# Norm statistics of two MLPs moved to a pinned place, GpSimd out of layer 1's projection, and the last square root on ScalarE

## The chip, the core and the metric

The kernel runs on one core of a Trainium2 chip, launched once. The metric is the device time of one execution in microseconds. The core's engines are TensorE (PE; PEld is its weight load), VectorE (DVE), ScalarE (ACT), GpSimd (POOL) and SyncE (SP, which issues the transfers here). Each engine runs its own instructions in their written order and waits at an instruction until what it needs is there.

## What is computed

A stream of 256 tokens of width 1024 goes through two blocks one after the other. All is float32. Cut to what matters here:

```python
def first_block(x, ...):
    for layer in range(2):
        h = rmsnorm(x, mix_norm[layer])
        if layer == 0:
            y = mixer_ab(h, ...)     # gated convolution beside attention
        else:
            y = mixer_c(h, ...)      # convolution, gated linear recurrence, projection c_w_out
        x = x + y
        x = x + sq_relu_mlp(rmsnorm(x, mlp_norm[layer]), w_up[layer], w_down[layer])
    return rmsnorm(x, final_norm)

def second_block(x, c, ctx, ...):
    h  = rmsnorm_2(x, norm_g) * (1 + scale) + shift      # shift, scale, gate from c and w_mod
    hc = rmsnorm_2(ctx, norm_g) * (1 + scale_c) + shift_c
    ...                                                  # two attentions over x and ctx
    y = (sigmoid(ga) * ya + sigmoid(gb) * yb) @ w_out
    return rmsnorm_2(x + gate * y, final_g)
```

`rmsnorm` divides a token by the root of the mean of its squares; `sq_relu_mlp` is `square(relu(h @ w_up)) @ w_down` with 4096 inner columns.

## The kernel before

Activations stand transposed: 128 channels on the partitions, 256 tokens along the row, eight such blocks for the width of 1024. Weights are read as 236 units of 128 x 1024 (512 KB) in the order of use. Each float32 operand is split into a rounded high half and the low half that is left, and a product is three matmuls (`mm3`, L383 to L385: high by high, low of the input by high, high by low of the weight), so a unit is 24 matmuls of 256 columns.

`fetch` issues a unit's transfer into one of four staging buffers (`raw`, `RAW = 4`). `prep` makes the halves: the high one (`wh`, or `wxh` where the second ring of buffers is in use) by ScalarE (L323) or by a cast on VectorE, the low one (`wl`, `wxl`) by VectorE or GpSimd (both L326). The table `POLICY` says for each kind of unit which engines do it: "av" is ScalarE then VectorE, "ag" ScalarE then GpSimd, "vv" VectorE for both. `unit` hands the next unit to a matmul loop and prepares units ahead; `more(n)` prepares n more at that place. `split` and `lo` (L435) do the same for activations.

An MLP (`mlp`) goes over 16 pairs of 256 inner columns. `up(p)` multiplies pair p; ScalarE applies ReLU (`mr`) and squares it into the high half (`mah`), GpSimd squares it again (`ma`, L989), VectorE takes the low half (`mal`). From pair 2 on, two rows of the down projection (of pair p - 2) follow each pair, summed in four accumulators. The norm of the MLP is applied at the end as its square, since ReLU squared is quadratic: `ssq` (L444, L445: ScalarE squares, GpSimd adds and folds) makes the channel sums of squares, `csum` (L452) sums over the partitions with two small matmuls, `meaneps` and a reciprocal give the factor, and `spread` multiplies it out over the partitions (L470) and copies it (`R2`).

During the first MLP VectorE also computes the conditioning vectors (`mod_setup`: L906 makes `cv`, L915 are 40 products with `w_mod`), hung in between as background steps; during the second one the context is normed the same way (`ctx_setup`, which calls `ssq` on `cx` in the same pool, where the tile `ssum` has one buffer).

Layer 1 (`layer1`) pins the order on TensorE and ScalarE between `conv` and `wrow(4)`. Gates, root (L1103), scan (L1108), GELU (L1115) and product (L1119, `done`) of four pairs of channel blocks alternate with the projections; then `wrow(k)` multiplies rows 0 to 4 of the output projection "wo1", and `proj_tail` rows 5 to 7, block pair by block pair, adding to `x` and making the next input halves `xsh` and `xsl`. Two of the four accumulators of "wo1" come free when VectorE has read `acc` at L1099.

At the end (`b2_out`) the squares of the result are summed by small matmuls into `st`; VectorE makes mean plus EPS (L458), GpSimd raises it to -0.5 (L463), TensorE spreads it (L470), VectorE multiplies, and five transfers write the output.

Tile schedules the instructions of every engine by itself unless `inorder` or `issue_after` fixes them; so a step that is written in one place may stand elsewhere in an engine's order.

## Time and profile before

| | before |
|---|---|
| median of 3 runs | 824.75 us (823.21 to 827.11) |
| profiled execution | 821.14 us |
| its span, first to last instruction | 819.4 us |
| granted TensorE clock, mean | 0.991 |
| TensorE busy | 787.9 us (96%) |
| VectorE busy | 576.4 us (70%) |
| ScalarE busy | 473.2 us (58%) |
| GpSimd busy | 199.0 us (24%) |

The table's last rows are shares of the span. A busy TensorE is not a TensorE at its peak, since matmuls overlap. Times in the views count from the start of the span. A share over the whole span says little of one stage; a stage is read from its own stretch of the timeline.

### The profile page before, as it was taken

What the parts mean: (1) busy time and instruction counts of PE and PEld (TensorE: products, weight loads), DVE (VectorE), ACT (ScalarE), POOL (GpSimd) and SP (SyncE); (2) the same over time, 40 slices, a digit from 0 to 9 for tenths busy, and PEclk for the clock granted to TensorE, in tenths of its full rate; (3) what the DMA queues carried; (4) which work ended last, traced back from release to release, by engine and by line L of the source; (5) the groups of instructions that cost most, each with busy time, mean ns of one, the idle gap of its engine ahead of it and who ended that gap; (6) DMA issues with size and microseconds to landing.
All of it is one profiled execution on the core that took longest, in us unless ns stands there. A gap on an engine that the chain in (4) does not pass through costs nothing.

```text
span 819.4 us, 16154 instructions
## 1 busy us (share of the span) xinstructions
PE 787.9 (96%) x6480; PEld 756.0 (92%) x6480; DVE 576.4 (70%) x952; ACT 473.2 (58%) x739; POOL 199.0 (24%) x151
## 2 busy tenths in 40 slices
PE   6999989999999999979999999999999999999996
PEld 5997889999999999978999999999989988889996
DVE  6999669999989787578746545557634877565843
ACT  5568656455545657877745444445626587765533
POOL 4796643011101202330531110111000022320001
PEclk9999999999999999999999999999999999999997
DMA  7874357787988832238726656664335533555531
GB/s 239 292 222 130 103 181 247 292 311 272 322 307 283 286 113 88 62 124 302 239 99 210 193 189 190 197 196 164 94 119 151 159 105 102 176 163 176 185 101 52
DMA packets 41259, 152.32 MB, mean 186 GB/s; under 512 B 4576, under 2 KB 5088, under 8 KB 39008
## 3 DMA queue, kind: packets, MB, share of 16 engines
q1 hardware_dynamic: 40752, 149.19, 55.5%
q10 hardware_dynamic: 432, 2.10, 0.7%
q8 instruction: 51, 0.84, 0.4%
q14 instruction: 24, 0.20, 0.1%
HBM read 149.17 MB, written 2.10 MB: 185 GB/s over the span
## 4 chain that ended last, share of the span: by engine, by line
PE 59%; issue 19%; DVE 8%; ACT 8%; POOL 4%; DMA 2%; SPq 0%; POOLq 0%; DVEq 0%; ACTq 0%
PE mm L383 10%; PE mm L384 10%; PE mm L385 10%; PE acc L384 7%; PE acc L383 7%; PE acc L385 7%; POOL ma L989 3%; PE acc L1423 2%; PE acc L1451 2%; PE mm L1460 2%; ACT wh L323 1%; DMA raw<-in_wst 1%; DVE wl L326 1%; PE mm L470 1%; DMA x<-in_xT 1%
## 5 line engine op out<-in xcount | busy, mean ns | idle before, releaser
L323 ACT ACTIVATE wh<-raw 128x1024 fp32r<-128x1024 f32 (+1 forms) x190 | 198.3, 1048 | 162.5 <-PE mm L384 64.2
L326 DVE TENSOR_TENSOR wl<-raw,wh 128x1024 fp32r<-128x1024 f32 (+1 forms) x159 | 197.6, 1250 | 100.1 <-ACT wh L323 98.3
L383 PE MATMUL mm<-xsh,wh 128*128 128x256 f32 x752 | 210.4, 280 | 0.0
L384 PE MATMUL mm<-xsl,wh 128*128 128x256 f32 x752 | 209.1, 278 | 0.0
L385 PE MATMUL mm<-xsh,wl 128*128 128x256 f32 x752 | 209.1, 278 | 0.0
L383 PEld LDWEIGHTS mm<-xsh,wh 128*128 128x128 f32 x752 | 141.7, 188 | 3.7 <-issue 3.3
L384 PEld LDWEIGHTS mm<-xsl,wh 128*128 128x128 f32 x752 | 141.7, 188 | 0.6 <-DVE xsl L878 0.2
L385 PEld LDWEIGHTS mm<-xsh,wl 128*128 128x128 f32 x752 | 141.3, 188 | 0.0
L989 POOL TENSOR_TENSOR ma<-mr 128x512 f32<-128x512 f32 x32 | 49.5, 1548 | 246.2 <-ACT mr L987 246.2
L384 PE MATMUL acc<-mal,wh 128*128 128x256 f32 x360 | 100.1, 278 | 1.0 <-DVE mal L435 1.0
L383 PE MATMUL acc<-mah,wh 128*128 128x256 f32 x360 | 100.3, 279 | 0.0
L385 PE MATMUL acc<-mah,wl 128*128 128x256 f32 x360 | 100.0, 278 | 0.0
L326 POOL TENSOR_TENSOR wl<-raw,wh 128x1024 fp32r<-128x1024 f32 x31 | 74.2, 2414 | 43.8 <-ACT wh L323 43.8
L323 ACT ACTIVATE wxh<-raw 128x1024 fp32r<-128x1024 f32 x47 | 49.2, 1055 | 38.8 <-DMA raw<-in_wst 34.9
L384 PEld LDWEIGHTS acc<-mal,wh 128*128 128x128 f32 x360 | 67.9, 189 | 1.2 <-DVE mal L435 1.2
L383 PEld LDWEIGHTS acc<-mah,wh 128*128 128x128 f32 x360 | 67.7, 188 | 0.0
L385 PEld LDWEIGHTS acc<-mah,wl 128*128 128x128 f32 x360 | 67.6, 188 | 0.0
L326 DVE TENSOR_TENSOR wxl<-raw,wxh 128x1024 fp32r<-128x1024 f32 x44 | 56.6, 1299 | 8.0 <-ACT wxh L323 8.0
L384 PE MATMUL mm<-xsl,wxh 128*128 128x256 f32 x208 | 58.1, 279 | 0.6 <-DVE xsl L878 0.6
L383 PE MATMUL mm<-xsh,wxh 128*128 128x256 f32 x208 | 58.3, 280 | 0.0
L385 PE MATMUL mm<-xsh,wxl 128*128 128x256 f32 x208 | 58.0, 279 | 0.0
L915 DVE CUSTOM_DVE_ANT_0 mdump<-mw,cv 128x1024 f32<-128x1024 f32 x40 | 48.7, 1217 | 2.7 <-DMA mw<-in_modw 2.6
(386 smaller groups left out, 1855.9 us busy)
## 6 DMA issues: line engine op xcount, KB each, us to landing
raw<-in_wst SPq DMA_DIRECT2D x240, 512.0 KB, 4.1
mw<-in_modw SPq DMA_DIRECT2D x12, 1024.0 KB, 7.2
nb<-in_nab SPq DMA_DIRECT2D x16, 256.0 KB, 3.7
ab<-in_alibi ACTq DMA_DIRECT2D x1, 1536.0 KB, 8.9
x<-in_xT SPq DMA_DIRECT2D x4, 256.0 KB, 4.9
cv<-in_cvec SPq DMA_DIRECT2D x1, 1024.0 KB, 4.7
cx<-in_cT SPq DMA_DIRECT2D x1, 1024.0 KB, 7.3
xd<-x SPq DMA_DIRECT2D x1, 1024.0 KB, 4.6
```

Of the source, the lines that this page charges most:

```text
L323: nc.scalar.activation(wh, r, AF.Copy)
L326: (nc.vector if lo == "v" else nc.gpsimd).tensor_tensor(wl, r, wh.bitcast(F32), op=ALU.subtract)
L383: mm(out, w[0], x[0], start=start, stop=False, skip_group_check=True)
L384: mm(out, w[0], x[1], start=False, stop=False, skip_group_check=True)
L385: return mm(out, w[1], x[0], start=False, stop=stop, skip_group_check=True)
L470: self.lasts = self.nc.tensor.matmul(ps[:, j * 128:(j + 1) * 128], rc[:, j:j + 1].to_broadcast([128, 128]), self.ident, start=True, stop=True)
L915: V.tensor_tensor_reduce(d, w, cv[:, s * 1024:(s + 1) * 1024], 0.5, 0.0, op0=ALU.mult, op1=ALU.add, accum_out=self.mod[:, s * 24 + i:s * 2 ...
L989: G.tensor_tensor(a, r, r, op=ALU.mult)
L1423: PE.matmul(sc[i], Q[tag, h][a][:, qs], K[tag, h][b], start=a + b == 0, stop=a == 1)
L1451: PE.transpose(pt[:, i * 128:(i + 1) * 128], P[:, i * 128:(i + 1) * 128], self.ident)
L1460: PE.matmul(o[64 * hh:64 * hh + 64, :T], vt[:, i, h * 64:h * 64 + 64], PTs[tag, h][:, i], start=i == 0, stop=i == 3, skip_group_check=True)
```

## The change

- `POLICY["wo1"]`: rows 0 to 2 get both halves from VectorE, rows 3 to 7 ScalarE and VectorE; before, rows 0 to 3 were ScalarE and GpSimd.
- In `layer1` the products `done(2)` and `done(3)` are written right after rows 0 and 1, and the units prepared there are put behind the low half that `done` makes.
- In `mlp` the squares of `x` are written at pair 1 (before: 4), their sum over the partitions and the reciprocal at pair 3 (before: 6), the spread before the second down row of pair 4 (before: at pair 8). TensorE's order in pairs 3 and 4 is pinned, and what those pairs issue afterwards is put behind the reciprocal.
- The spread of the final gain (`R1`) moves from the output stage to the end of `b2_kv`.
- At the end ScalarE takes the square root of mean plus EPS, ahead of the last four scalings; VectorE takes the reciprocal. The table with the root is loaded early, behind the last tanh.

```diff
--- before.py
+++ after.py
@@ -45,7 +45,7 @@
 POLICY.update(val=("av", "ag", "av", "ag"), gate=("av", "av", "av", "ag"), xr=("av",), ri=("av",), cg=("av", "av", "av", "av", "ag", "ag", "ag", "ag"))
 POLICY["wo0"] = ("ag",) * 7 + ("av",)
 POLICY["up"] = ("ag",) * 4 + ("av",) * 60
-POLICY["wo1"] = ("ag",) * 4 + ("av",) * 4
+POLICY["wo1"] = ("vv",) * 3 + ("av",) * 5
 PADC = 30
 
 COLS = {}
@@ -432,7 +432,7 @@
         self.nc.vector.scalar_tensor_tensor(l, xs, g, h.bitcast(F32), op0=ALU.mult, op1=ALU.subtract)
 
     def lo(self, l, src, h):
-        self.nc.vector.tensor_tensor(l, src, h.bitcast(F32), op=ALU.subtract)
+        self.lastlo = self.nc.vector.tensor_tensor(l, src, h.bitcast(F32), op=ALU.subtract)
 
     def ssq(self, pool, x3):
         nc = self.nc
@@ -1000,17 +1000,22 @@
                 self.ahead = min(2 * p - 14, 13)
             if l == 1 and p == 4:
                 self.wx, self.slot = None, 0
-            up(p)
-            if p == 4:
-                parts = self.ssq(mp, x)
-            if p == 6:
-                v = self.meaneps(self.csum(parts), D)
-                rv = self.t(self.cp, [128, 2], "rv")
-                V.reciprocal(rv, v)
-            if p == 8:
-                R2 = self.spread(mp, rv, "R2")
-            if p >= 2:
-                for k in (2 * p - 4, 2 * p - 3):
+            with ExitStack() as order:
+                if p == 3 or p == 4:
+                    order.enter_context(self.inorder(PE.engine))
+                if p == 4:
+                    order.enter_context(self.tc.issue_after(ri_.ins))
+                up(p)
+                if p == 1:
+                    parts = self.ssq(mp, x)
+                if p == 3:
+                    v = self.meaneps(self.csum(parts), D)
+                    rv = self.t(self.cp, [128, 2], "rv")
+                    ri_ = V.reciprocal(rv, v)
+                    order.enter_context(self.tc.issue_after(ri_.ins))
+                for k in (2 * p - 4, 2 * p - 3) if p >= 2 else ():
+                    if k == 5:
+                        R2 = self.spread(mp, rv, "R2")
                     self.krow(acc, self.unit("down"), A.pop(k), k == 0, False)
         for k in range(28, 32 - NT):
             self.krow(acc, self.unit("down"), A.pop(k), False, False)
@@ -1162,13 +1167,17 @@
             gelu(3)
             self.more(2)
             acc = [self.ps("acc") for _ in range(4)]
-            for k in range(4):
-                if k == 2:
-                    done(2)
-                if k == 3:
-                    done(3)
+            wrow(0)
+            done(2)
+            with self.tc.issue_after(self.lastlo.ins):
+                self.more(1)
+            wrow(1)
+            done(3)
+            with self.tc.issue_after(self.lastlo.ins):
+                self.more(2)
+            for k in (2, 3):
                 wrow(k)
-                self.more(1 if k == 0 else 2)
+                self.more(2)
             wrow(4)
         self.ahead = 2
         xs = self.new_h()
@@ -1360,6 +1369,7 @@
                 V.scalar_tensor_tensor(cf[:, k], cf[:, k], self.p("gcq", k), RQ, op0=ALU.mult, op1=ALU.mult)
                 self.split(cf[:, k], cq[0][:, k], cq[1][:, k])
         zpair("za", 1, ep, cqn)
+        d["R1"] = self.spread(bp, d["r1"], "R1")
         d.update(kb=kb, vb=vb, krh=krh, krl=krl, ck=ck, wk=wk, va=va, bp=bp)
         q8 = self.t(self.cp, [128, 2112], "hch")[:, :2048].rearrange("p (a b) -> p a b", a=8)
         for i in range(2):
@@ -1492,7 +1502,7 @@
         def gdone(nm, p):
             def f(ps):
                 tg[nm, p] = self.t(bp, [128, 512], f"t{nm}", bufs=2)
-                S.activation(tg[nm, p], ps, AF.Tanh, scale=0.5)
+                self.lastt = S.activation(tg[nm, p], ps, AF.Tanh, scale=0.5)
             return f
 
         def gpair(nm, p):
@@ -1561,14 +1571,17 @@
             V.tensor_tensor(y, y, tg["gb", p], op=ALU.add)
             self.split(self.pair(y), ys[0][:, 2 * p:2 * p + 2], ys[1][:, 2 * p:2 * p + 2])
             if p == 1:
-                R1 = self.spread(op, d["r1"], "R1")
                 for k in range(8):
-                    V.scalar_tensor_tensor(x[:, k], x[:, k], self.p("fin", k), R1, op0=ALU.mult, op1=ALU.mult)
+                    V.scalar_tensor_tensor(x[:, k], x[:, k], self.p("fin", k), d["R1"], op0=ALU.mult, op1=ALU.mult)
         def orow(w, k, ms, end):
             for m in ms:
                 o = last[:, :T] if m == 7 else acc[m // 2][:, (m % 2) * T:(m % 2 + 1) * T]
                 c = slice(m * 128, m * 128 + 128)
                 self.mm3(o, (w[0][:, c], w[1][:, c]), yrow(k), k == 0 and (m % 2 == 0 or m == 7), end)
+        eps = self.t(op, [128, 1], "eps")
+        G.memset(eps, EPS)
+        with self.tc.issue_after(self.lastt.ins):
+            S.activation(self.warm, self.warm, AF.Sqrt)
         for k in range(6):
             orow(self.unit("wo2"), k, range(8), False)
         ws = [self.unit("wo2") for _ in range(2)]
@@ -1581,7 +1594,8 @@
                           stop=end, skip_group_check=True)
         def scale(b):
             for k in (2 * b, 2 * b + 1):
-                S.activation(x[:, k], x[:, k], AF.Copy, scale=self.p("fg2", k))
+                i = S.activation(x[:, k], x[:, k], AF.Copy, scale=self.p("fg2", k))
+            return i
 
         def fold(b):
             (G if b < 2 else V).tensor_tensor(sq[b][:, 0], sq[b][:, 0], sq[b][:, 1], op=ALU.add)
@@ -1601,14 +1615,20 @@
         with self.tc.issue_after(xi.ins):
             fold(2)
         with self.tc.issue_after(si.ins):
-            for b in range(1, 4):
-                scale(b)
+            sc = scale(1)
         stat(sq[0][:, 0], True)
         stat(sq[1][:, 0])
         stat(sq[3][:, 0])
         stat(sq[2][:, 0])
         stat(sq[3][:, 1], end=True)
-        RF = self.across(self.rsq(self.meaneps(st[:, :2], D)))
+        sd = self.t(op, [128, 2], "sd")
+        with self.tc.issue_after(sc.ins):
+            sd_ = S.activation(sd, st[:, :2], AF.Sqrt, scale=1.0 / D, bias=eps)
+        with self.tc.issue_after(sd_.ins):
+            scale(2)
+            scale(3)
+        V.reciprocal(sd, sd)
+        RF = self.across(sd)
         for i, (k0, k1) in enumerate(((0, 1), (1, 3), (3, 5), (5, 7), (7, 8))):
             xb = x[:, k0:k1]
             V.tensor_tensor(xb, xb, self.b2(RF, k1 - k0), op=ALU.mult)
```

The order on the engines moves at three places. First VectorE in layer 1, from the last gate product to the first new `gl` (`ig`, `th`, `gl`: recurrence tiles of eight blocks; `wl_4301`, `wl_4374`, `wl_4439`: low halves of rows 0 to 2 of "wo1"). Before:

```order
L1087 SCALAR_TENSOR_TENSOR ig_3753<-ig_3753,acc_4098 128x256 x2
L1106 TENSOR_TENSOR ig_3753<-ig_3753,th_3752 128x512 x2
L1108 SCALAR_TENSOR_TENSOR th_3752<-r_3751,ig_3753 128x256 x4
L1112 TENSOR_TENSOR gl_3754<-mm_4242,R_3826 128x512
L1119 TENSOR_TENSOR th_3752<-th_3752,gl_3754 128x512 x2
L435 TENSOR_TENSOR ysl_3747<-th_3752,xr_4292 128x512
```

And now:

```order
L1092 SCALAR_TENSOR_TENSOR ig_3753<-ig_3753,acc_4098 128x256
L325 CAST wh_4300<-raw_4298 128x1024
L1092 SCALAR_TENSOR_TENSOR ig_3753<-ig_3753,acc_4098 128x256
L325 CAST wh_4373<-raw_4371 128x1024
L326 TENSOR_TENSOR wl_4301<-raw_4298,wh_4300 128x1024
L326 TENSOR_TENSOR wl_4374<-raw_4371,wh_4373 128x1024
L1111 TENSOR_TENSOR ig_3753<-ig_3753,th_3752 128x512 x2
L1113 SCALAR_TENSOR_TENSOR th_3752<-r_3751,ig_3753 128x256 x4
L1117 TENSOR_TENSOR gl_3754<-mm_4242,R_3826 128x512
L1124 TENSOR_TENSOR th_3752<-th_3752,gl_3754 128x512
L325 CAST wh_4438<-raw_4436 128x1024
L1124 TENSOR_TENSOR th_3752<-th_3752,gl_3754 128x512
```

Two casts and two low halves stand ahead of the root's first product (`ig` by `th`), a third cast between two products; its low half follows behind the next `ysl`. The four GpSimd rows of these units are gone.

Second, VectorE at the start of the first MLP, from the last unit of the second pair (`cv` is the conditioning vector, `mal` the low half of a squared pair, `var` and `rv` the statistic). Before:

```order
L326 TENSOR_TENSOR wl_1500<-raw_1497,wh_1499 128x1024
L906 SCALAR_TENSOR_TENSOR cv_1439<-mw_1441,cv_1439 128x2048
L326 TENSOR_TENSOR wl_1583<-raw_1580,wh_1582 128x1024
L326 TENSOR_TENSOR wl_1613<-raw_1610,wh_1612 128x1024
L435 TENSOR_TENSOR mal_1566<-ma_1564,mah_1565 128x512
```

And now, with the rows around the statistic:

```order
L326 TENSOR_TENSOR wl_1500<-raw_1497,wh_1499 128x1024
L326 TENSOR_TENSOR wl_1595<-raw_1592,wh_1594 128x1024
L326 TENSOR_TENSOR wl_1625<-raw_1622,wh_1624 128x1024
L435 TENSOR_TENSOR mal_1566<-ma_1564,mah_1565 128x512
...
L458 TENSOR_SCALAR var_1792<-mm_1789 128x2
L1014 RECIPROCAL rv_1794<-var_1792 128x2
L326 TENSOR_TENSOR wxl_1799<-raw_1796,wxh_1798 128x1024
L435 TENSOR_TENSOR mal_1784<-ma_1782,mah_1783 128x512
L326 TENSOR_TENSOR wxl_1829<-raw_1826,wxh_1828 128x1024
L326 TENSOR_TENSOR wxl_1860<-raw_1857,wxh_1859 128x1024
L906 SCALAR_TENSOR_TENSOR cv_1439<-mw_1441,cv_1439 128x2048
```

The row of `cv` has gone from ahead of the first rows' splits to behind the statistic, and the splits of the fifth pair (`wxl_1799`, `wxl_1829`) stand behind the reciprocal.

Third, GpSimd in the second MLP (`ssum` holds the sums of squares, of the context or of `x`; `rc` is the context's root). Before, the first sums are the context's:

```order
L444 TENSOR_TENSOR ssum_4995<-ssum_4995,sqt_5003 128x512
L989 TENSOR_TENSOR ma_4844<-mr_4843 128x512
L445 TENSOR_TENSOR ssum_4995<-ssum_4995 128x256
L989 TENSOR_TENSOR ma_4852<-mr_4851 128x512
L989 TENSOR_TENSOR ma_4921<-mr_4920 128x512
L989 TENSOR_TENSOR ma_5062<-mr_5061 128x512
L463 TENSOR_TENSOR rc_5171<-var_5169,mhalf_85 128x2
```

And now, the first sums being those of `x`:

```order
L445 TENSOR_TENSOR ssum_4859<-ssum_4859 128x256
L989 TENSOR_TENSOR ma_4844<-mr_4843 128x512
L989 TENSOR_TENSOR ma_4852<-mr_4851 128x512
L989 TENSOR_TENSOR ma_4933<-mr_4932 128x512
L989 TENSOR_TENSOR ma_5074<-mr_5073 128x512
L444 TENSOR_TENSOR ssum_5007<-ssum_5007,sqt_5009 128x512
L444 TENSOR_TENSOR ssum_5007<-ssum_5007,sqt_5012 128x512
L444 TENSOR_TENSOR ssum_5007<-ssum_5007,sqt_5015 128x512
L445 TENSOR_TENSOR ssum_5007<-ssum_5007 128x256
L463 TENSOR_TENSOR rc_5190<-var_5188,mhalf_85 128x2
```

The context's sums have moved behind the product of the fourth pair (`ma_5074`), next to the root that needs them; on TensorE their small matmuls stand after the first unit of the fifth pair.

## Rows read from the trace of the kernel before

**Rows 1.** The page: span, TensorE's busy row, VectorE's 40 slices of 20.5 us.

```profile
span 819.4 us, 16154 instructions
...
PE 787.9 (96%) x6480; PEld 756.0 (92%) x6480; DVE 576.4 (70%) x952; ACT 473.2 (58%) x739; POOL 199.0 (24%) x151
...
DVE  6999669999989787578746545557634877565843
```

**Rows 2.** Waits of TensorE: us in total, times, longest.

```profile
PE acc L385 <- POOL wl L326: 2.9, 2, 1.5
```

**Rows 3.** Timeline, TensorE, layer 1: start, duration, instruction, [idle before, releaser].

```profile
351.57 0.39 PE L383 MATMUL acc<-xr,wh 128*128 128x256 f32 x1 [0.67 <-DVE th L1099]
...
354.26 0.58 PE L385 MATMUL acc<-xr,wl 128*128 128x256 f32 x1 [1.47 <-POOL wl L326]
...
360.05 0.39 PE L385 MATMUL acc<-xr,wl 128*128 128x256 f32 x1 [1.45 <-POOL wl L326]
...
367.42 0.39 PE L384 MATMUL acc<-ysl,wh 128*128 128x256 f32 x1 [1.57 <-DVE ysl L435]
...
372.60 0.39 PE L384 MATMUL acc<-ysl,wxh 128*128 128x256 f32 x1 [0.94 <-DVE ysl L435]
...
380.08 0.28 PE L383 MATMUL mm<-xsh,wxh 128*128 128x256 f32 x1
```

**Rows 4.** Busy us by stretch in layer 1, all engines; PEclk is the granted clock.

```profile
353.70:357.10 3.40, 2.84 (x13) 2.84 (x14) 2.93 (x5) 3.37 (x5) 0.51 (x1) 0.51 0.39 134
```

**Rows 5.** Timeline, VectorE, layer 1.

```profile
337.11 1.29 DVE L1106 TENSOR_TENSOR ig<-ig,th 128x512 f32<-128x512 f32 x2 [2.90 <-ACT th L1103]
...
350.83 0.69 DVE L1099 SCALAR_TENSOR_TENSOR th<-acc,th 128x512 f32<-128x512 f32 x1 [0.36 <-ACT acc L1098]
...
357.73 5.63 DVE L1119 TENSOR_TENSOR th<-th,gl 128x512 f32<-128x512 f32 x2
363.28 1.21 DVE L326 TENSOR_TENSOR wl<-raw,wh 128x1024 fp32r<-128x1024 f32 x1
```

**Rows 6.** Timeline, GpSimd, layer 1.

```profile
334.78 2.41 POOL L326 TENSOR_TENSOR wl<-raw,wh 128x1024 fp32r<-128x1024 f32 x1 [4.18 <-ACT wh L323]
...
357.62 5.19 POOL L326 TENSOR_TENSOR wl<-raw,wh 128x1024 fp32r<-128x1024 f32 x2 [3.42 <-ACT wh L323]
```

**Rows 7.** Timeline, ScalarE, layer 1.

```profile
342.56 1.05 ACT L323 ACTIVATE wh<-raw 128x1024 fp32r<-128x1024 f32 x1
...
350.73 1.04 ACT L323 ACTIVATE wh<-raw 128x1024 fp32r<-128x1024 f32 x1
351.79 1.28 ACT L1103 ACT_TABLE_LOAD   x1
```

**Rows 8.** Timeline, VectorE, second block: a cast of half a unit.

```profile
594.79 0.42 DVE L1326 CAST wkh<-wh 128x512 fp32r<-128x512 f32 x1
```

**Rows 9.** Timeline, VectorE and TensorE, start of the first MLP.

```profile
123.12 2.39 DVE L906 SCALAR_TENSOR_TENSOR cv<-mw,cv 128x2048 f32<-128x2048 f32 x1 [3.66 <-ACT mw L905]
...
130.67 0.38 PE L384 MATMUL acc<-mal,wh 128*128 128x256 f32 x1 [1.03 <-DVE mal L435]
```

**Rows 10.** Timeline, GpSimd and TensorE, second MLP.

```profile
388.97 5.99 POOL L444 TENSOR_TENSOR ssum<-ssum,sqt 128x512 f32<-128x512 f32 x3 [26.16 <-PE mm L385]
...
417.74 0.51 PE L452 MATMUL mm<-ones,ssum 128*128 128x1 f32 x4
...
419.20 4.02 POOL L444 TENSOR_TENSOR ssum<-ssum,sqt 128x512 f32<-128x512 f32 x3
```

**Rows 11.** Timeline, GpSimd, TensorE and ScalarE at the end; a small ScalarE row earlier.

```profile
811.32 0.71 POOL L463 TENSOR_TENSOR rc<-var,mhalf 128x2 f32<-128x2 f32 x1 [2.69 <-DVE var L458]
...
812.08 1.22 PE L470 MATMUL mm<-ident,rc 128*128 128x128 f32 x4 [1.04 <-POOL rc L463]
...
805.39 0.42 ACT L1596 ACTIVATE csq<-xo 128x256 f32<-128x256 f32 x1 [11.76 <-DVE xo L1595]
...
137.94 0.21 ACT L936 ACTIVATE sm<-sm 128x8 f32<-128x8 f32 x1
```

## The prediction

> **What bounds the kernel now.** I read the page first. TensorE is busy for 787.9 of 819.4 us in 6480 matmuls [rows 1], 0.122 us for one, so a change can only win back the stretches in which TensorE waits, and every new wait on it costs its full length. The waits of TensorE come second: the low halves of weights that GpSimd makes cost 2.9 us in two waits [rows 2]. The timeline of TensorE shows where these and the others lie: five of them within 22 us in layer 1's projection, before the second MLP starts at 380.08 [rows 3]: 0.67 for an accumulator, 1.47 and 1.45 for GpSimd's splits of rows 1 and 2, 1.57 and 0.94 for VectorE's low halves of the inputs of rows 4 and 6. In the middle of it the granted clock is 0.51 [rows 4], the 1.2 GHz level, after TensorE had waited twice.
>
> What ends last there is a chain of ScalarE and VectorE. ScalarE makes its cast for row 1 at 350.73, then loads a table, takes the root [rows 7]; VectorE then runs root and scans, and its last two products, two of the kind that cost 1.29 at 337.11, take 5.63 [rows 5], because GpSimd splits two units at that time (5.19 us) [rows 6]. So **VectorE's products wait for GpSimd's splits, whole instructions at a time**.
>
> **Layer 1.** Removed: four ScalarE/GpSimd splits, of rows 0 to 3. Added: three casts and three low halves on VectorE (rows 0 to 2), and row 3 as ScalarE cast with VectorE split. A split's low half costs 1.21 on VectorE [rows 5]. No cast of this size is in the trace; half of it took 0.42 [rows 8]; I take 0.7, bounded above by the 1.21 of a low half and below by 0.42.
> The rows of the order show where they stand. Two casts and two low halves come before the root's first product, where VectorE now idles 2.90 us [rows 5]: 2 x 0.7 + 2 x 1.21 = 3.8. The one GpSimd split that stays there (2.41, from 334.78) [rows 6] shuts the two low halves out, so 3.8 + 2.4 is 6.2 us, begun some 0.7 before the idle stretch: the root's product starts about 2.7 late. The third cast and low half fall where VectorE waits for ScalarE's tanhs and cost nothing; without that cover, 1.9. ScalarE gets rid of the casts at 342.56 and 350.73 (1.05 and 1.04) ahead of the table load at 351.79 [rows 7]: 2.7 - 2.1, so the load starts 0.6 late. From here it turns: the products start at 357.73 + 0.6 and take 1.29 in place of 5.63, done at 359.6 and not 363.4. Row 3's low half (1.21) follows, 360.8; the remaining 22 matmuls of row 3 take 2.7, row 4's 24 take 2.9 (its own halves are there by 362.7), so row 4 ends at 366.4. Before, its third matmul ran at 367.42 [rows 3], and 22 more end at 370.1: **3.7 earlier**. The wait of 0.94 in the tail falls away too, since row 6's input is made by about 363.5: 4.6, and with the small one before it **4.7 us**.
> The first wait, for the accumulator, gets longer: it ends with VectorE's row at 350.83 + 0.69 [rows 5], now 0.6 later; the clock may fall again, but TensorE then waits for row 3's low half anyway. Bounds: casts at 1.21 put 1.0 and 0.5 more on the chain, 3.2 us of gain; if the two low halves fitted beside GpSimd's split, 2.4 more, 7.1.
> The Trainium skill, SBUF — State Buffer, section on who interferes with whom, says that VectorE and GpSimd share a port pair as an exclusive lock, held for a whole instruction, by VectorE when it has two SBUF inputs, and that a cast can take it too. For two-input rows the trace agrees (5.63 beside 5.19, against 1.29); for casts no row here shows it. By that rule the casts queue with the GpSimd split as my sum has it; without it the chain would be about 0.4 us shorter.
>
> **First MLP.** The order moves the product of the conditioning vector (2.39 at 123.12) [rows 9] from ahead of two splits and the first low half to behind the statistic. TensorE waited 1.03 for that half at 130.67 [rows 9]. 2.39 is more than 1.03, so the wait goes: **1.0 us**, bounds 0 (GpSimd's product for it bounds it) and 1.03. The statistic's two small matmuls, reciprocal and spread only move. VectorE now stands at the statistic until the fourth pair is done, and behind it queue the splits of the fifth pair and the next rows; TensorE has two rows, 48 x 0.122 = 5.9 us, before it needs the first of them, which takes 1.21. That covers it; without it, up to 1.2.
>
> **Second MLP.** The same pinning, but here the sums of x now come first, and the context's share their one buffer: ScalarE's first square of the context waits for the statistic's matmul, and GpSimd's three additions and the fold come only after the fourth pair's product. TensorE wants the context's sum 72 matmuls after the statistic, 8.8 us. Before, it was asked at 417.74 [rows 10] and nobody waited. GpSimd's chain is now: about 0.6 for the ReLU ahead (0.42 for half that width [rows 11]), a product, three additions, a fold of half the size. Alone an addition takes 4.02 / 3 = 1.34; beside two splits three took 5.99 [rows 10], 2.0 each. Alone: 0.6 + 4.5 x 1.34 = 6.6, no wait. At 2.0: 9.6, a wait of 0.8. But the splits that queued behind the statistic run just then; with one low half ahead of each, 0.6 + 5 x 2.55 = 13.4, a wait of 4.6. I take a **loss of 1.3**, nearer the row beside two splits, and keep 0 and 4.6.
>
> **The end.** The last matmuls wait 1.04 for GpSimd's power (0.71) [rows 11]; the other 0.33 is VectorE's affine step and the hops, whose place the reciprocal takes. A ScalarE row of eight columns took 0.21 [rows 11]: 0.71 - 0.21 = 0.5 at best, 0.3 if the root costs the 0.42 of a wider row. I take **0.45**. The four scalings moved behind it still end before the last VectorE rows need them. The added table load, 1.28 by [rows 7], lies where ScalarE idles 11.76 us before 805.39 [rows 11]: nothing.
> The Trainium skill, ScalarE: Activation LUTs, section on what a table load costs, has about 2.7 us for a load. The trace has 1.28; even by the page's figure the idle stretch hides it, so the sum would be the same.
> The spread of the final gain moves from the output stage to an earlier one, four matmuls and one ScalarE row each: 0.
>
> **Sum:** -4.7 - 1.0 + 1.3 - 0.45 = -4.85, say 4.9. The profiled execution took 821.14, so 816.2; the median of the runs shown, 824.75, lies 3.6 above it, so on that scale **819.9**. About 0.5%, 4.1 us, can be told from no change.
>
> **Rivals.** *VectorE becomes layer 1's bound.* For it: three casts and four low halves, up to 8.5 us, on the engine that ends the chain. Against: it idles 2.90 and more between rows there. Casts at 1.21 and a wait of 1.8 in the second MLP: -3.2 - 1.0 + 1.8 - 0.45 = -2.9, **821.9**.
> *The head start is given back in the second MLP.* TensorE reaches it 4.7 earlier, but its weights come through four staging buffers freed by VectorE's splits, and the context's sum ends by GpSimd's chain. With the wait at 4.0: -4.7 - 1.0 + 4.0 - 0.45 = -2.2, **822.6**.
> *VectorE stands still at the pinned statistics, and the kernel gets slower.* All four staging buffers can hold units whose splits queue behind the reciprocal; then no transfer starts until it is done. If VectorE's stand is not made up in the first MLP, up to the 5.9 us of two rows, and in the second the wait is 4.6: 5.9 + 4.6 - 4.7 - 0.45 = +5.4, **830.2**. It decides once a split comes later than 5.9 us after the statistic. For it: VectorE's digit is 9 or 8 in all but one slice of the first MLP (123 to 266 us) [rows 1]; against: only 1.21 stands directly between.
> *The projection's waits only move*, because ScalarE's chain and not GpSimd bounds the accumulator: the gain would be the tail and the first MLP, 1.5, **823.3**.
>
> **Chances.** Forecast 0.60; VectorE the bound 0.16; given back 0.10; slower 0.07; only moved 0.07. The forecast's own range is 817.0 to 822.5. With the bounds and all rivals but the slower one: **816.5 to 824.5**. Of the forecast's 0.60 about 0.49 lies past 4.1 us, and 0.04 of the VectorE rival: faster 0.53, same 0.40, slower 0.07.
>
> **What would show it.** Right: no TensorE wait for GpSimd's splits in layer 1, the two products at about 1.3, row 4 ending some 4 us earlier, and the second MLP's start at about 374.4 (4.7 and 1.0 earlier than 380.08); no wait at the first MLP's first row; a wait before the context's sum of 0 to 2 us; the last four matmuls after a wait near 0.6. Wrong: a wait for the accumulator of 3 us or more, a context sum over 3 us late, or TensorE waiting for splits after either statistic.

## The result, and the profile after

| kernel | median us (range, runs) | ratio to the kernel before [95% interval] |
|---|---|---|
| before | 823.98 (821.57 to 827.11, 4) | 1 |
| changed | 835.76 (830.99 to 837.64, 4) | 1.0144 [1.0113, 1.0175] |

The change makes the kernel slower by 1.4%, 11.8 us. The prediction had 819.9, with a range up to 824.5: wrong in sign. The profiled execution after took 837.18 us, its span is 835.4, 16.0 longer than before [rows 1]. The page of the changed kernel, span and busy row:

```profile
span 835.4 us, 16135 instructions
...
PE 797.0 (95%) x6480; PEld 764.5 (92%) x6480; DVE 583.8 (70%) x959; ACT 472.0 (57%) x739; POOL 189.5 (23%) x147
```

The medians differ by 11.8; what follows is read from these two executions. TensorE has as many matmuls as before, 9.1 us more busy time and about 7 us more idle time [rows 1]. So only part of the loss is waiting; the rest is matmuls that take longer. The waits of TensorE after (us in total, times, longest):

```profile
PE acc L383 <- ACT mah L988: 4.2, 2, 3.5
PE acc L384 <- DVE mal L435: 4.0, 2, 2.9
...
PE acc L383 <- DVE th L1104: 1.9, 2, 1.2
PE mm L383 <- ACT xsh L872: 1.7, 1, 1.7
PE mm L452 <- POOL ssum L445: 1.7, 1, 1.7
...
PE acc L385 <- DVE wl L326: 1.0, 1, 1.0
PE mm L384 <- DVE xsl L878: 1.0, 2, 0.6
PE mm L470 <- DVE sd L1630: 0.7, 1, 0.7
```

GpSimd's splits of layer 1 [rows 2] are gone, as forecast. The halves of squared pairs (`mah`, `mal`) are waited for 8.2 us, before 1.9; new are also 1.7 for the inputs of the second MLP and 1.7 for the context's sum.

Because both kernels issue the same matmuls, the start of each matmul can be compared with that of the matmul with the same number before. The difference, after minus before, changes here:

| stretch | change, us |
|---|---|
| start-up to the first MLP | +2.1 |
| first MLP up to its last two pairs | -3.3 |
| last two pairs of the first MLP and its down projection | +12.4 |
| layer 1 up to "wo1" | -0.1 |
| "wo1", to the first matmul of the second MLP | -6.05 |
| first 108 matmuls of the second MLP | +4.7 |
| next 300 (statistic, context's sum, spreads) | +3.1 |
| next 1080 of the second MLP | +3.95 |
| rest | -0.6 |

The first line isn't the change's: nothing of it stands there, and over the traces of all kernels here the first MLP starts anywhere from 112.8 us, as in this trace of the kernel before, to 119.8. Of the second line's 3.3, 1.3 is the wait at 130.67 [rows 9] with the matmuls right behind it. The other 2.0 is pace, of which more below: the kernel before ran some 570 matmuls of this stretch at 117.8 ns from start to start and the rest at 113.3, the changed one some 120.

**Layer 1** is what was forecast. VectorE in it, after (the low halves of rows 0 and 1, the root's products, the third cast, the last two products):

```profile
345.99 4.56 DVE L326 TENSOR_TENSOR wl<-raw,wh 128x1024 fp32r<-128x1024 f32 x2
350.47 1.28 DVE L1111 TENSOR_TENSOR ig<-ig,th 128x512 f32<-128x512 f32 x2
...
355.21 0.68 DVE L325 CAST wh<-raw 128x1024 fp32r<-128x1024 f32 x1
...
369.15 1.27 DVE L1124 TENSOR_TENSOR th<-th,gl 128x512 f32<-128x512 f32 x2
```

A cast costs 0.68 (0.7 taken), the two low halves ahead of the root's product 4.56 beside GpSimd's one remaining split, and the last two products 1.27 in place of 5.63 [rows 5]. From the first matmul of "wo1" (359.57) to the first of the second MLP (385.10) it is 25.5 us; before, 31.6.

**The end of the first MLP** is where most of the loss is. TensorE after, and the stretches (busy us, matmuls, then granted clock):

```profile
280.67 0.38 PE L383 MATMUL acc<-mah,wh 128*128 128x256 f32 x1 [0.69 <-ACT mah L988]
283.94 0.57 PE L384 MATMUL acc<-mal,wh 128*128 128x256 f32 x1 [2.89 <-DVE mal L435]
290.16 0.58 PE L383 MATMUL acc<-mah,wxh 128*128 128x256 f32 x1 [3.51 <-ACT mah L988]
291.89 0.58 PE L384 MATMUL acc<-mal,wxh 128*128 128x256 f32 x1 [1.16 <-DVE mal L435]
```

```profile
284.00:297.60 13.60, 8.93 (x38) 8.34 (x39) 8.70 (x10) 5.85 (x9) 1.59 (x1) 0.50 0.78 263
```

Four waits make 8.25 us (before, 0.84 at this place), and the 38 matmuls of the next 13.6 us run at a granted clock of 0.50, the 1.2 GHz level: 8.93 us where 38 at the pace around them (0.113) would take 4.3. 7.4 more waiting and 4.6 for the clock are 12.0 of the 12.4.

Where do the waits come from? ScalarE makes `mah` after casts that wait for their units (`wh<-raw`; after, ScalarE, ahead of the longest wait), VectorE makes `mal` behind low halves and products with `w_mod`.

```profile
285.93 1.06 ACT L323 ACTIVATE wh<-raw 128x1024 fp32r<-128x1024 f32 x1 [1.68 <-DMA raw<-in_wst]
287.90 1.06 ACT L323 ACTIVATE wh<-raw 128x1024 fp32r<-128x1024 f32 x1 [0.92 <-DMA raw<-in_wst]
...
289.48 0.63 ACT L988 ACTIVATE mah<-mr 128x512 fp32r<-128x512 f32 x1
```

The products with `w_mod`, and the transfers for them, in the kernel before and after (line, engine, count, shortest/median/longest ns, first and last start). Before:

```profile
L912 SPq DMA_DIRECT2D mw<-in_modw x12: 327/426/1222, 119.9 to 244.6; - x12
...
L915 DVE CUSTOM_DVE_ANT_0 mdump<-mw,cv x40: 1173/1218/1226, 133.5 to 254.7; 128x1024 f32<-128x1024 f32 x40
```

After:

```profile
L912 SPq DMA_DIRECT2D mw<-in_modw x12: 327/374/967, 122.0 to 267.0; - x12
...
L915 DVE CUSTOM_DVE_ANT_0 mdump<-mw,cv x40: 1168/1218/1227, 152.2 to 277.3; 128x1024 f32<-128x1024 f32 x40
```

The first of the 40 products starts 18.7 us later, the last 22.6, and eleven of the twelve transfers of `w_mod` 9 to 25 us later, the last by 22.4. VectorE then waits for them at the very end of the MLP, with the splits of the prefetched units queued behind:

```profile
142.91 0.16 DVE L458 TENSOR_SCALAR var<-mm 128x2 f32<-128x2 f32 x1 [4.67 <-PE mm L452]
...
148.60 2.28 DVE L906 SCALAR_TENSOR_TENSOR cv<-mw,cv 128x2048 f32<-128x2048 f32 x1
...
268.78 1.23 DVE L915 CUSTOM_DVE_ANT_0 mdump<-mw,cv 128x1024 f32<-128x1024 f32 x1 [2.18 <-DMA mw<-in_modw]
```

The conditioning product waits for the pinned reciprocal and starts at 148.60, not 123.12 [rows 9]; all 40 products and every `w_mod` transfer but the first follow it. In SyncE's order the last two `w_mod` transfers stood behind 80 and 82 issues of weights (those of L316); now behind 89 and 91. From pair 9 on the kernel prefetches up to 13 units, so they now meet that prefetch.

### The profile page after: what moved, and what is told of

It is laid out like the page before. It is cut to its first block, busy times and chain, and to the rows that moved or that the text cites. A ratio compares the mean times of both kernels' runs of the same rounds, so it can differ in the third digit from the quotient of the medians.

```text
span 835.4 us, 16135 instructions
## 1 busy us (share of the span) xinstructions
PE 797.0 (95%) x6480; PEld 764.5 (92%) x6480; DVE 583.8 (70%) x959; ACT 472.0 (57%) x739; POOL 189.5 (23%) x147
## 4 chain that ended last, share of the span: by engine, by line
PE 75%; DVE 10%; ACT 5%; issue 3%; DMA 3%; POOL 2%; SPq 0%; DVEq 0%; ACTq 0%; POOLq 0%
PE mm L383 13%; PE mm L384 13%; PE mm L385 13%; PE acc L384 9%; PE acc L383 9%; PE acc L385 9%; PE acc L1433 2%; DMA mw<-in_modw 2%; PE acc L1461 2%; PE mm L1470 2%; DVE wl L326 2%; DVE wxl L326 1%; DMA raw<-in_wst 1%; DVE ysl L435 1%; POOL ssum L444 1%
## 5 line engine op out<-in xcount | busy, mean ns | idle before, releaser
L323 ACT ACTIVATE wh<-raw 128x1024 fp32r<-128x1024 f32 (+1 forms) x187 | 195.1, 1048 | 183.3 <-PE mm L384 66.0
L326 DVE TENSOR_TENSOR wl<-raw,wh 128x1024 fp32r<-128x1024 f32 (+1 forms) x163 | 205.8, 1269 | 113.4 <-ACT wh L323 108.3
L989 POOL TENSOR_TENSOR ma<-mr 128x512 f32<-128x512 f32 x32 | 47.8, 1494 | 267.1 <-ACT mr L987 255.9
L326 POOL TENSOR_TENSOR wl<-raw,wh 128x1024 fp32r<-128x1024 f32 x27 | 64.5, 2418 | 29.1 <-ACT wh L323 28.8
```

Source lines behind the costliest of these rows:

```text
L323: nc.scalar.activation(wh, r, AF.Copy)
L326: (nc.vector if lo == "v" else nc.gpsimd).tensor_tensor(wl, r, wh.bitcast(F32), op=ALU.subtract)
L989: G.tensor_tensor(a, r, r, op=ALU.mult)
```

## The experiments

A flag per MLP chooses the place of its norm; the pins, the `issue_after` and the spread hang on the same flag. The short diffs below are against the changed kernel, unless another is named.

```diff
+            new = l in NORMS            # changed kernel: (0, 1)
...
-                if p == 1:
+                if p == (1 if new else 4):
                     parts = self.ssq(mp, x)
-                if p == 3:
+                if p == (3 if new else 6):
```

| run | median us | ratio to before [95%] |
|---|---|---|
| e1_early_cond | 831.06 | 1.0075 [1.0039, 1.0111] |
| e2_norms_alone | 838.05 | 1.0164 [1.0098, 1.0231] |
| e3_layer1_alone | 819.96 | 0.9976 [0.9941, 1.0011] |
| e4_no_norms | 819.01 | 0.9948 [0.9913, 0.9982] |
| e5_norm_second | 826.57 | 1.0048 [1.0017, 1.0080] |
| e6_second_spread | 825.60 | 1.0030 [1.0001, 1.0060] |
| e7_norm_first | 827.39 | 1.0060 [1.0031, 1.0088] |
| e8_up_gpsimd | 820.86 | 0.9996 [0.9959, 1.0032] |
| e9_first_early_modw | 822.17 | 0.9985 [0.9955, 1.0014] |
| e10_second_two_bufs | 826.53 | 1.0054 [1.0030, 1.0079] |
| e11_two_bufs_spread | 826.96 | 1.0062 [1.0035, 1.0089] |
| e12_mended | 828.63 | 1.0090 [1.0058, 1.0121] |
| e13_spread_between | 820.39 | 0.9952 [0.9928, 0.9975] |
| e14_mended_between | 821.16 | 0.9967 [0.9938, 0.9996] |
| e15_no_norms_again | 817.54 | 0.9931 [0.9900, 0.9961] |

The runs e1 to e4, e5 to e8, e9 to e12 and e13 to e15 were made together, each group against runs of the kernel before on the same chip (medians 822.09, 823.02, 821.77, 823.36). Comparisons across groups go by the ratios.

### Which part costs: e2, e3, e4

e2_norms_alone: the kernel before with `NORMS = (0, 1)` and nothing else.

> The kernel before with only the move of the two MLP norms to the pinned place. Theory (the norms alone make the loss): about +10.4 us at the end of the first MLP, and +1.7 to +3.7 at the context's sum in the second, together 11 to 14 slower than before, median 835 to 838. Rival (the loss needs the new split of layer 1 or its earlier end as well): under 4 us slower than before, median below 828.

e3_layer1_alone: the kernel before with

```diff
-POLICY["wo1"] = ("ag",) * 4 + ("av",) * 4
+POLICY["wo1"] = ("vv",) * 3 + ("av",) * 5
```

and the new order of `done` and `wrow`.

> The kernel before with only the new split of layer 1's output projection and the products done(2), done(3) written earlier. Theory (the head start of 5 to 6 us that the projection gains is mostly lost at the start of the second MLP, where weights arrive too late and VectorE's addition to x queues behind their low half): projection ends 5 to 6 us sooner, waits of 2 to 3 us for the input halves and 1.7 us at half clock behind them, net -1 to -3, median 821 to 823. Rival (the give-back comes only with the moved norms): net -4 to -6, median 818 to 820.

e4_no_norms: `NORMS = ()`.

> The changed kernel with both MLP norms put back where they were; layer 1's split, the moved spread of the final gain and the final root on ScalarE stay. Theory: as the layer 1 part alone, and 0.3 to 0.7 less for the final root (wait of the last matmuls 0.70 against 1.04), median 820.5 to 822.5. Rival (something in the other parts costs time too): median above 824.

Measured: the norms alone cost 1.64%, as much as the whole change within the interval; without them it is 0.5% faster than before. All the loss is in the moved norms. The medians of e3 and e4 lie under the theories' ranges, 819.96 under 821 to 823 and 819.01 under 820.5 to 822.5; but against the 822.09 of the kernel before beside them e3's 2.1 us is the theory's -1 to -3, and not the rival's -4 to -6. Layer 1 alone gains 0.24% with an interval that reaches 1: of the 6.0 us that its projection gains in the trace, 3.4 are left 108 matmuls into the second MLP. There TensorE waits for the input halves (e3, TensorE):

```profile
374.41 0.38 PE L384 MATMUL mm<-xsl,wxh 128*128 128x256 f32 x1 [0.34 <-DVE xsl L878]
...
376.93 0.39 PE L384 MATMUL mm<-xsl,wxh 128*128 128x256 f32 x1 [0.60 <-DVE xsl L878]
...
379.58 0.38 PE L383 MATMUL mm<-xsh,wxh 128*128 128x256 f32 x1 [1.09 <-ACT xsh L872]
```

because VectorE's addition to `x` stands behind low halves of units still on their way (after, VectorE):

```profile
382.53 1.22 DVE L326 TENSOR_TENSOR wxl<-raw,wxh 128x1024 fp32r<-128x1024 f32 x1 [1.70 <-ACT wxh L323]
383.67 0.68 DVE L863 TENSOR_TENSOR x<-x,acc 128x512 f32<-128x512 f32 x1
```

e8_up_gpsimd tried to free that queue: e4 with

```diff
-POLICY["up"] = ("ag",) * 4 + ("av",) * 60
+POLICY["up"] = ("ag",) * 4 + ("av",) * 28 + ("ag", "av") * 2 + ("av",) * 28
```

> The kernel without the moved norms, with the low halves of the first and third weight units of the second MLP made by GpSimd, so that VectorE's additions to x in the projection's tail no longer queue behind low halves of units that are still in transfer. Theory (that queue makes the waits of 0.6, 1.35 and 0.14 us at the start of the second MLP and the half clock behind them, 1.7): 1 to 3 us faster than without, median 816 to 818. Rival (GpSimd's 2.4 us splits come too late or shut VectorE out): 0 to 3 us slower, median 819 to 822.

Measured 820.86, no gain over e4: a miss, in the rival's range. TensorE now waits 0.48, 1.74 and 0.86 for `xsl` at this place, 3.1 in all against e4's 2.1. The waits moved; what would remove them stays open.

### The two norms apart: e7, e5

e7_norm_first: `NORMS = (0,)`.

> The changed kernel with the norm of the second MLP put back; that of the first stays at the pinned place. Theory (the twelve transfers of w_mod stand up to nine weight units later in SyncE's order, and the last two meet the deep prefetch at the end of the first MLP): 9 to 12 us slower than the kernel without both moved norms (819.0), median 828 to 831. Rival (the loss at the end of the first MLP needs the second MLP's order too): under 3 us slower, median below 822.

e5_norm_second: `NORMS = (1,)`.

> The changed kernel with the norm of the first MLP put back; that of the second stays at the pinned place. Against the kernel without both moved norms (819.0): theory (a wait of 1.7 us for the context's sum, 1.7 us of half clock behind it, and the slow pace of TensorE, 117.8 ns from matmul to matmul in place of 113.3, for about 1000 matmuls behind the two spreads, 4.5 us): 6 to 8 us slower, median 825 to 827. Rival (the pace is chance and differs from execution to execution): only the wait and the clock, 2 to 3.5 us slower, median 821 to 822.5.

Against e4's 0.9948, the first MLP's norm costs 1.1% (9 us) and the second's 1.0% (8 us); together 2.1%, and the whole change lies 2.0% above e4. So the two losses add up, within the intervals. e7's median (827.39) is 0.6 under the forecast's range, and its trace shows the same waits as after: 0.46, 2.49, 3.54 and 1.16. e5's 826.57 is within its range.

### The first MLP: e1, e9

e1_early_cond: the conditioning steps begin four steps sooner.

```diff
-        self.bg += no * 12 + [silu]
+        self.bg += no * 8 + [silu]
```

> The changed kernel, with the background step that makes the conditioning vector written four steps sooner, so that its product stands on VectorE ahead of the pinned statistic again; all else as in the change. Theory A (the pinned reciprocal holds back the conditioning product by 25.5 us, and so the 40 products with w_mod and the last transfers of w_mod until they collide with the prefetch at the end of the first MLP): the waits of 0.69, 2.89, 3.51 and 1.16 us at the end of the first MLP and the stretch at half clock behind them go, 10 to 12 us less than the changed kernel, median 824 to 827. Theory B (VectorE's stand at the statistic itself stops the transfers, DMA share 0.34 in 140 to 150 us, and the first MLP never makes that up): the stand is still there, so at most 3 us less, median 832 or more.

Measured 831.06: 0.7% less than the changed kernel, half of what theory A had, and in neither theory's range. In its trace the waits of 0.69 and 2.89 are gone and those of 2.83 and 1.15 remain, and in SyncE's order the last `w_mod` transfer still stood behind 89 issues of weights. So moving the conditioning product alone doesn't settle it; the transfers must come earlier too.

e9_first_early_modw: `NORMS = (0,)` and

```diff
-        self.bg += no * 12 + [silu]
+        self.bg += no * 6 + [silu]
...
-            if i % 3 == 2:
-                self.bg += no
```

> As the kernel with only the first MLP's norm moved, and the background steps of the conditioning vectors begin six steps sooner and without the eight pauses, so that SyncE issues the last two w_mod transfers ahead of weight units 77 and 82, as before the change, and not of 90 and 92. Theory (the late w_mod transfers are the whole loss at the end of the first MLP): the waits there fall from 7.65 us to under 1.5 and no half clock follows, median 818 to 821, 6 to 10 us below that kernel. Rival (VectorE's stand at the pinned statistic is what is never made up): less than half of it comes back, median 824 or more.

Measured: 0.75% below e7, 6 us, two thirds of the loss. The rival asked for less than half and falls. e9 brings the 40 products forward together with their transfers; which of the two holds up the splits isn't separated. The median, 822.17, is 1.2 above the forecast's range, and the waits fall to 3.5 us and not under 1.5. TensorE in e9:

```profile
287.83 0.38 PE L383 MATMUL acc<-mah,wxh 128*128 128x256 f32 x1 [2.16 <-ACT mah L986]
289.56 0.58 PE L384 MATMUL acc<-mal,wxh 128*128 128x256 f32 x1 [1.35 <-DVE mal L435]
```

In e15, which moves no norm, the same two matmuls wait 0.78 and 1.36; of e12 and e14 below, both with e9's first MLP, neither waits in e12, and in e14 they wait 1.12 and 1.35. So this place is sensitive from execution to execution, and e9's remaining 0.4% over e4 isn't explained by one trace, the less so as that trace is the slowest of its twelve executions (825.84). One part has a row: the repair takes back the gain that was forecast. With the conditioning product ahead of the splits again, the wait of 1.03 at the first low half [rows 9] is there in e9, e12 and e14 (1.02, 1.03 and 1.03).

### The second MLP: e6, e10, e11, e13

e5's trace has the context's sum 1.73 late and a stretch at half clock behind it, and then something that no wait shows: TensorE takes longer per matmul at full granted clock. Matmuls in the same 60 us of the second MLP, in before, after and e5 (one fence each; the count is in brackets):

```profile
490.00:550.00 60.00, 60.00 (x532) 1.00 0.63 193
```

```profile
490.00:550.00 60.00, 60.00 (x512) 1.00 0.61 189
```

```profile
490.00:550.00 60.00, 60.00 (x512) 1.00 0.60 186
```

In the trace a matmul lasts 0.28 us and overlaps the next, so a count takes in two or three that only reach into the stretch; from start to start the trace has 113.3 ns where 60 us count 532, and 117.8 where they count 512. So TensorE has two paces, both at a granted clock of 1.00, the 2.4 GHz level; in the traces it goes from one to the other at a wait or at the small matmuls of a statistic, with few exceptions, and then keeps it. For some 1100 matmuls behind the second MLP's spreads the slow one costs 5 us.

The pace can differ between executions of one kernel, as e5's rival had it, but not everywhere. e4 and e15 are the same kernel; the 40 us ahead of the first MLP's column sum in e4, then in e15:

```profile
134.00:174.00 40.00, 40.00 (x342) 1.00 0.84 300
```

```profile
134.00:174.00 40.00, 40.00 (x355) 1.00 0.82 301
```

e4 had waited 0.18 at the first low half and went on slow, e15 1.04 and went on fast. Behind a wait, then, the pace isn't fixed by the kernel (the kernel before was slow here, e3 with the same order on TensorE fast, both behind 1.03). Behind the sums and spreads of both MLPs e4 and e15 agree.

e6_second_spread: e5, and the spread once more at pair 6.

```diff
-                if p == 8 and not new:
+                if p == 8 and not new or p == 6 and new:
                     R2 = self.spread(mp, rv, "R2")
```

> As the kernel with only the second MLP's norm moved, and the spread of the factor done a second time two pairs later (four small matmuls and one ScalarE row more, the same values). Theory (a spread turns the slow pace of TensorE into the fast one and the other way round): the matmuls behind it start 113.3 ns apart, about 980 of them, 4.4 us less, 0.5 more for the spread itself, so 3 to 4.5 us faster than that kernel, median 821 to 823. Rival (the pace does not hang on the spread): 0.5 us slower than that kernel.

Measured 825.60: a miss. Its trace shows why: here TensorE, unlike in e5, was fast already behind the factor's first spread, and the second spread put it on the slow pace. Stretches of e6 ahead of and behind that second spread (113 and 118 ns from start to start):

```profile
427.00:444.00 17.00, 17.00 (x153) 1.00 0.57 172
447.00:550.00 103.00, 103.00 (x876) 1.00 0.60 187
```

e6 waited as long for the context's sum as e5 (1.72 and 1.73), but in e6 no half clock followed, and its context's spread came after a wait of 0.54 that e5 hasn't. Whether either made the difference isn't shown.

e10_second_two_bufs: e5, and the context's sums get a buffer of their own.

```diff
-        s = self.t(pool, [128, 2, T], "ssum")
+        s = self.t(pool, [128, 2, T], "ssum", bufs=2)
```

> As the kernel with only the second MLP's norm moved, and the sums of squares have two buffers, so that the context's sums no longer wait for those of x. Theory (the shared buffer makes the wait of 1.73 us and the half clock behind it; the slow pace behind the two spreads stays): the wait goes, 2 to 3.5 us faster than that kernel, median 822.5 to 825. Rival (GpSimd's chain is late whatever the buffer): no difference over 1 us.

Measured 826.53 (1.0054, e5 1.0048): no gain, a miss. The wait for the context's sum went, and a new one came, since the context's additions now stand ahead of a pair's product on GpSimd (e10, TensorE):

```profile
398.73 0.39 PE L384 MATMUL acc<-mal,wh 128*128 128x256 f32 x1 [2.09 <-DVE mal L435]
```

e11_two_bufs_spread: e10 with e6's second spread.

> As the kernel with two buffers for the sums of squares, and the second MLP's spread done a second time two pairs later. Theory (each spread turns TensorE's pace round, a column sum sets it to 117.8 ns; behind two column sums and two spreads it is slow, behind the third spread fast; no wait disturbs it here): 113.3 ns behind it for about 980 matmuls, 3 to 4.5 us faster than the kernel with two buffers, median 819 to 821. Rival (the pace after a spread is chance): no difference over 1.5 us.

Measured 826.96: a miss. Behind the second spread the pace stayed slow. A spread does not simply turn the pace round: e6 and e11 together end that theory.

What was left is the sequence. In every trace with sum, sum, spread, spread in the second MLP (after, e1, e2, e5, e6, e10, e11, e12) TensorE has 511 or 512 matmuls in those 60 us (in e6 only behind its additional spread); in every one with sum, spread, sum, spread (before, e3, e4, e7, e8, e9) it has 532. e13_spread_between puts that sequence back while the norm stays at the pinned place: e10, and

```diff
+                if p == 4 and new and l == 1:
+                    R2 = self.spread(mp, rv, "R2")
                 up(p)
...
-                    if k == 5 and new:
+                    if k == 5 and new and l == 0:
```

> As the kernel with only the second MLP's norm moved and two buffers for the sums, and the spread of the factor stands ahead of the context's column sum, so that the small matmuls come as sum, spread, sum, spread, as they did before the change, and not as sum, sum, spread, spread. Theory (in this sequence the last spread has left TensorE at 113.3 ns in every trace without the moved norm): fast from there to the end of the second MLP, about 1170 matmuls, 4 to 5 us faster than the kernel with two buffers, median 821 to 823. Rival (the slow pace comes from the pinned place or something else in the moved norm): it stays at 117.8, no difference over 1.5 us.

Measured 820.39, 0.9952 [0.9928, 0.9975], 1.0% below e10. Stretches of e10: behind the first sum (slow), behind the context's spread (fast), behind the factor's spread (slow):

```profile
411.00:418.00 7.00, 7.00 (x62) 1.00 0.60 178
422.60:424.90 2.30, 2.30 (x23) 1.00 0.76 228
426.00:466.00 40.00, 40.00 (x342) 1.00 0.62 186
```

And of e13: behind the first sum (slow), and behind the context's spread, which is now the last (fast):

```profile
411.00:416.00 5.00, 5.00 (x45) 1.00 0.29 105
...
423.60:463.60 40.00, 40.00 (x355) 1.00 0.61 199
490.00:550.00 60.00, 60.00 (x532) 1.00 0.60 192
```

342 matmuls in 40 us became 355. Matmul by matmul e13 gains 5.0 us on e10 behind the spreads, as the pace gives, and the profiled span fell from 823.1 to 818.6. The medians show 6 to 8; the rest isn't explained. e10's twelve times lie in two groups, six from 822.1 to 825.1 and six from 828.0 to 833.4, and its trace is of the first; no trace shows what the second group has. The rival, a pace set by the pinned place, falls.

### The whole change mended: e12, e14, and the version without: e15

e12_mended: the whole change with e9's early steps, two buffers and the spread done twice.

> The whole change with three repairs: the conditioning steps begin six steps sooner without pauses, two buffers for the sums of squares, the second MLP's spread done twice. Theory (these three things were all that the moved norms cost): no slower than the kernel without the moved norms, median 817 to 820. Rival (the pinning costs something more): median above 822.

Measured 828.63, a miss: the waits at the end of the first MLP were gone in its trace, but the pace was slow in both MLPs (in the first, 512 matmuls in 200 to 260 us, where after has 532). In the first MLP two matmuls, at 153.2 and 153.4 us, start 0.22 us behind the one before them, with no wait on record; from there TensorE was fast, and the spread left it slow.

e14_mended_between: the same with e13's place of the spread instead of the second spread.

> The whole change with the conditioning steps six steps sooner and without pauses, two buffers for the sums and the second MLP's spread ahead of the context's column sum. Theory (late w_mod transfers, the shared buffer and the pace are what the moved norms cost): 4 to 5 us faster than the repair with the spread done twice (828.6), median 822 to 825. Rival: as that one, 827 or more.

Measured 821.16, 0.9967 [0.9938, 0.9996], just under the forecast. Late `w_mod` transfers and the sequence of the small matmuls, then, are nearly all that the moved norms cost: 1.0144 became 0.9967. Against e12 alone this isn't a clean comparison: its trace was slow in the first MLP too, which is worth some 5 us, and e14's, with the same order on TensorE there, was fast. The second buffer only moved a wait.

e15_no_norms_again: `NORMS = ()` as in e4.

> The changed kernel without the moved norms again, beside these two. Its gain over the kernel before should repeat: 2.5 to 4 us, ratio 0.995 to 0.997.

Measured 817.54, 0.9931 [0.9900, 0.9961], better than forecast. This is the version that beats both kernels, in two groups of runs: keep the new split of "wo1", the final root and the earlier spread of the final gain, and leave the norms where they were. Even mended, moving them gains nothing that these runs can show.

## Why the prediction was wrong, step by step

**Layer 1, right.** Predicted -4.7, measured -6.05 to the start of the second MLP. The terms hold: the cast 0.7 (0.68), the product of the root 2.7 late (2.3, at 350.47 against 337.11 and the 11.06 that the kernel is late by then), the last two products 1.29 (1.27), and no wait for GpSimd. The wait for the accumulator got longer, 1.23 and 0.68 for 0.67. A new wait of 1.02 for a low half (`wl`) is the one that the text saw for row 3. The clock stayed at full speed here, which is worth about the extra 1.3: before, 13 matmuls took 2.84 us at 0.51 [rows 4], 1.4 more than 13 at 0.113. The sum had left that open ("the clock may fall again").
The Trainium skill, SBUF — State Buffer, section on who interferes with whom: for a low half beside a GpSimd split the trace agrees again (two low halves 4.56 in all, against 2.4 uncontended, while GpSimd's split of 2.49 ran); the one cast beside that split, 0.68 at 345.39, had begun 0.45 before it, so what the section has of casts is not shown here.

**First MLP, wrong, and the largest error.** The text said that the wait of 1.03 would go, since the product of the conditioning vector moves behind the statistic. It went: TensorE waits for nothing from 130 to 280 us, and 1.3 of the 3.3 in the table is this term. The 2.0 of pace beside it no term had; as e4 and e15 differ there, it is luck in the main. But the step "the statistic's two small matmuls, reciprocal and spread only move", with one split behind VectorE's stand, left out what else hangs on the moved product: 40 products on VectorE and eleven transfers in SyncE's queue. The order of SyncE was not followed to its end; it shows the last two transfers nine weight issues later. e7 prices this at 9 us, e9 gets 6 back.

**Second MLP, wrong.** A loss of 1.3 was taken, bounds 0 to 4.6; the term priced the wait for the context's sum and nothing behind it. The wait itself was sized well: 1.73, with three additions in 6.22 us behind the fourth pair's product, 2.1 each where 2.0 was taken. Left out were the clock, which fell to half behind that wait (1.7 us in the table's 3.1), and the pace, about 5 us. e5 prices the whole at 8.

**The end, right.** The last wait is 0.70 for 1.04: 0.34, inside 0.3 to 0.5. The four matmuls behind it took 0.68, before 1.22 at half clock [rows 11], a gain that no term had; in e8, with the new end, they took 1.19, so it isn't the change's for certain.

```profile
828.62 0.68 PE L470 MATMUL mm<-ident,sd 128*128 128x128 f32 x4 [0.70 <-DVE sd L1630]
```

**The rivals.** "The head start is given back" (0.10) is what layer 1's gain met, with its mechanism: 4.7 us came back in the first 108 matmuls of the second MLP after, 2.6 in e3. "VectorE stands still at the pinned statistics" (0.07) had the sign, and 830.2 is its nearest price, but not the mechanism: VectorE stood 4.67 at the statistic and TensorE waited for no split behind it. The cost came 140 us later, through the background chain. (Its reading of rows 1 is a slip: the digit is 9 or 8 in all seven slices from 123 to 266 us.) Of the prediction's signs of being wrong none appeared, neither a long wait for the accumulator nor a context's sum over 3 us late nor a wait for splits behind a statistic: the loss lay where it had named no sign.

## What to carry to other kernels

When an instruction is pinned behind another, list what depends on the moved one to the end of its chain, on every queue: here one product drew 40 more and eleven transfers with it, and the price was paid 140 us later, where the schedule had put its prefetch. A wait on TensorE has a price beyond its length: where the clock falls behind it, the matmuls of the next stretch cost nearly double (0.213 us from start to start, where 0.113 was the pace). And when two versions differ by less than a per cent, count matmuls per stretch before looking for a cause in the waits, and in more than one trace of a kernel, since the pace can differ between executions.

## What the hardware showed that was not expected

TensorE ran the same kind of matmul, 256 columns, at 113.3 or at 117.8 ns from start to start, at a granted clock of 1.00 in both cases (532 and 512 matmuls in 60 us). In the second MLP the sequence of the statistics went with it, in one trace of each of 17 runs: sum, spread, sum, spread ended fast in all nine, sum, sum, spread, spread slow in seven of eight; e6 was fast behind it, until its additional spread. In the first MLP all 17 were slow behind the sum and 16 fast behind the spread; the other is e12, which something had made fast ahead of the spread. It is not the whole rule: a further spread turned fast to slow in e6 and left slow as it was in e11 and e12, and behind a wait two executions of one kernel, e4 and e15, went on at different paces. What in the chip sets the pace stays open.
The Trainium skill, TensorE: Matmul & The Clock Gate, section on the back-to-back issue gap, gives the columns divided by 2.4 GHz plus 2.5 ns for a matmul by itself, by an estimate from it 109.2 at 256 columns, and for a stream of weight loads and matmuls about 81 ns at 128 columns and 131 at 512: one pace for each, and none for 256 in a stream. The measurement decides: 113.3 and 117.8, above the first and between the other two.
